# A decoder kernel: the values' first block product placed behind the gates' last one on TensorE

## The chip, the cores and the metric

One core of a Trainium2 chip runs the kernel. The core has five engines that run side by side, each with its own queue of instructions that it works through in order: TensorE (PE, matrix products; its weight loads are listed apart as PEld), VectorE (DVE), ScalarE (ACT), GpSimd (POOL) and SyncE (SP), which issues transfers. They meet through semaphores. The metric is the time of one execution on the device in microseconds.

## The reference

The kernel computes two layers of a decoder on 512 tokens of width 1024, in float32. The part that matters here is the retention branch of a layer, with its gates and values:

```
z = rmsnorm(x, g_mix) @ w_in                # split into ... rq, rk, rv, rg, ga, gb
r = chunkwise_retention(rotate(rq), rotate(rk) * 128 ** -0.5, rv)   # 4 heads, values 256 wide
r = r * rsqrt(mean(r * r, -1) + eps)
yb = (r.reshape(B, S, 1024) * silu(rg)) @ w_b
x = x + (sigmoid(ga) * (A @ w_a) + sigmoid(gb) * yb) @ w_out
```

rg are the retention's gates and rv its values; each is one block of 1024 columns of the combined projection. A is the attention's output.

## The kernel before, in words

Every float32 product is done as three matmuls on rounded parts: each operand is split into hi (a rounded copy, ScalarE, L342 for weights) and lo (the rest, VectorE, L343), and hi x hi, hi x lo and lo x hi are added up in PSUM. The function products (L394 to L396) issues such triples and keeps its last matmul in latest[0].

Weights come in units of 128 x 1024, in the fixed order of unit_order. A call of unit() hands out the next unit and, with it, traces the split of the unit three places ahead (SPLIT = 3) and the load of one four further on (AHEAD = 4). The split tiles hi and lo have four buffers each, so a new split waits until the products of an older unit are done.

Some large products are made from seven smaller block products in place of eight. For the gates' second half this is last_gates, for the values it is values. Both hold three accumulators: a, b and c (one PSUM bank each in last_gates, two each in values; the pool ps_mm has five banks, ps_aux three). Each has seven calls of multiply: a from the first quarter of the inputs; b begins as ScalarE's copy of a; c and b take products with combinations of the inputs that the class Turned has built before; keep copies a bank away with ScalarE; put reads a bank with VectorE and writes a result. Later multiplies go on adding into the same bank, so such a reader stands between two products. In last_gates a multiply is 24 matmuls of 128 x 256 (L1015) with one unit of weights; in values it is 24 matmuls of 128 x 512 with two units.

The order in last_gates is: a; copy to b; c; keep(c) (L1026); b; keep(b); a; put(0, 0) (L1036); c; put(0, 1) (L1033 and L1034); the silu of two gates (L1062, L1063); b; put(1, 1) (L1033, L1034); b; put(1, 0). In values the first call is multiply(a, quarter(0, 0)), which needs only the scaled inputs xh and xl and the first two units of values' weights; then come the copies of a into b (L969) and the second call, on c. A dummy matmul (L929) opens one of the banks of b.

A layer calls last_gates and then values directly after it; before them is the product with w_a (group w_a, 128 x 512), after them the projections qk(2) and qk(3), with the retention of the first two heads drawn in beside them.

The order in the code is not the order in the queues. After tracing, a planner runs the program forward in a simulated time of its own: on each engine it takes, among the instructions whose operands and buffers are ready, the one that was traced first. The result is each engine's fixed queue. An instruction that waits in that queue holds up all behind it. The context issue_after(ins) adds an edge of order only: what is traced inside it, on the engine of ins, comes behind ins in that queue. Instructions for other engines that are traced inside are not bound.

Of the kernel before, what the change touches and what calls it, by code (L numbers as in the profile page):

```python
# [111 lines left out]
def view(slot):  # L112
    return slot[0][:, slot[1], :]
# [3 lines left out]
def decoder(ctx, tc, xT, x_first, w_in, w_rg, w_rv, w_a, w_b, w_wo, w_up, w_pair, w_down, w_end, tables, decay, band, g_last, out):  # L117
    nc = tc.nc
# [10 lines left out]
    def f32(ap):  # L129
        return ap.bitcast(F32)  # L130

    def temp(name="t"):
        return tmp.tile([P, T], F32, tag="t", name=name, bufs=7)
# [4 lines left out]
    def bank(pool, name):  # L138
        return pool.tile([P, T], F32, tag=pool.name, name=name)
# [112 lines left out]
    def pace(src):  # L252

        if quiet[0]:
            return
        pace_count[0] += 1
        if steps and pace_count[0] % 2 == 0:
            mark = small.tile([P, 1], F32, tag="mark", name="mark", bufs=2)
            ins = nc.gpsimd.tensor_copy(mark, src[:, 0:1])
            with tc.issue_after(ins.ins):  # L260
                if next(steps[0], DONE) is DONE:
                    steps.pop(0)
# [91 lines left out]
    def unit(name, layer):  # L354
        i = state["next"]
        assert order[i][:2] == (layer, name), (order[i], layer, name)
        state["next"] += 1
        hold = state["hold"]
        split_until(i + SPLIT + 1 if hold is None else max(i + 1, min(hold, i + SPLIT + 1)))
        return parts.pop(i)  # L360
# [27 lines left out]
    def products(ps, pairs, start, stop, resume=False):  # L388


        n = len(pairs)
        for i, ((ah, al), (bh, bl)) in enumerate(pairs):
            more = {"skip_group_check": True} if resume else {}
            nc.tensor.matmul(ps, ah, bh, start=start and i == 0, stop=False, **more)  # L394
            nc.tensor.matmul(ps, ah, bl, start=False, stop=False, **more)  # L395
            latest[0] = nc.tensor.matmul(ps, al, bh, start=False, stop=stop and i == n - 1, **more).ins  # L396

    latest, behind, spread = [None], [], []
# [15 lines left out]
    def split(hi, lo, src, scale=None):  # L414

        if scale is None:
            up = nc.scalar.activation(hi, src, AF.Copy)  # L417
            down = nc.vector.tensor_tensor(lo, src, f32(hi), ALU.subtract)  # L418
        else:
            up = nc.scalar.activation(hi, src, AF.Copy, scale=scale)  # L420
            down = nc.vector.scalar_tensor_tensor(lo, src, scale, f32(hi), ALU.mult, ALU.subtract)
        return up.ins, down.ins
# [198 lines left out]
    def layer_body(layer):  # L621
# [299 lines left out]
        def quarter(half, tokens):  # L921
            at = slice(tokens * H, tokens * H + H)
            return [(xh[:, k, at], xl[:, k, at]) for k in range(4 * half, 4 * half + 4)]

        def values(turned):

            a, c = ([bank(ps_mm, "rv") for _ in range(2)] for _ in range(2))
            b = [bank(pool, "rv") for pool in (ps_mm, ps_aux)]
            nc.tensor.matmul(b[1], ones, xh[:, 0, :], start=True, stop=True)  # L929
            plus, minus = rms_mix.columns, small.tile([P, NB], F32, tag="ncol", name="ncol", bufs=1)  # L930
            nc.vector.tensor_scalar(minus, plus, -1.0, None, ALU.mult)

            def multiply(ps, moving, start=True):
                for u in range(2):
                    hi, lo = unit("rv", layer)
                    for m in range(2):
                        at = slice(m * P, (m + 1) * P)
                        pairs = []
                        for k in range(2):
                            xh_, xl_ = moving[2 * u + k]  # L940
                            cols = slice(k * T, (k + 1) * T)
                            pairs.append(((xh_[:, at], xl_[:, at]), (hi[:, cols], lo[:, cols])))
                        products(ps[m], pairs, start and u == 0, u == 1, not start)

            def scale(j, m, sign):
                return (plus if sign > 0 else minus)[:, 2 * j + m : 2 * j + m + 1]

            def keep(j, ps, sign):
                got = []
                for m in range(2):  # L950
                    t = temp("kept")
                    nc.scalar.activation(t, ps[m], AF.Copy, scale=scale(j, m, sign))
                    got.append(t)
                return got

            def put(i, j, ps, sign, kept=None):
                for m in range(2):
                    hi, lo = slots.one(), slots.one()
                    if kept:
                        nc.vector.scalar_tensor_tensor(kept[m], ps[m], scale(j, m, sign), kept[m], ALU.mult, ALU.add)  # L960
                        split(view(hi), view(lo), kept[m])
                    else:
                        split(view(hi), view(lo), ps[m], scale(j, m, sign))
                    rv[i, 2 * j + m] = (hi, lo)
                    pace(f32(view(hi)))

            multiply(a, quarter(0, 0))
            for m in range(2):
                nc.scalar.activation(b[m], a[m], AF.Copy)  # L969
            multiply(c, turned[1])  # L970
            five = keep(1, c, -1)
            multiply(b, turned[2], False)
            turned.free(0)
            two = keep(1, b, 1)
            multiply(a, quarter(1, 0), False)
            quiet[0] = False
            put(0, 0, a, 1)
            multiply(c, quarter(1, 1), False)
            put(0, 1, c, 1, two)
            multiply(b, turned[3], False)  # L980
            put(1, 1, b, -1, five)
            multiply(b, turned[4], False)
            turned.free(1)
            put(1, 0, b, -1)
# [19 lines left out]
        def last_gates(turned):  # L1004

            a, b, c = (bank(ps_mm, "rg") for _ in range(3))
            two = [big("z") for _ in range(2)]

            def multiply(ps, moving, start=True):
                hi, lo = unit("rg", layer)  # L1010
                for k, (vh, vl) in enumerate(moving):
                    for n in range(2):
                        o, cols = ps[:, n * H : (n + 1) * H], slice((2 * k + n) * P, (2 * k + n + 1) * P)
                        for w, v in ((hi, vh), (hi, vl), (lo, vh)):
                            nc.tensor.matmul(  # L1015
                                o,
                                w[:, cols],
                                v,
                                start=start and k == 0 and n == 0 and w is hi and v is vh,
                                stop=k == 3 and n == 1 and w is lo,  # L1020
                                skip_group_check=True,
                            )

            def keep(ps, sign):
                t = temp("kept")
                nc.scalar.activation(t, ps, AF.Copy, scale=float(sign))  # L1026
                return both(t)

            def put(i, j, ps, sign, kept=None):
                v = two[i][:, :, TOKENS[j]]  # L1030
                by = rstd()[:, TOKENS[j]].unsqueeze(1).broadcast_to([P, 2, H])
                if kept is not None:
                    nc.vector.scalar_tensor_tensor(kept, both(ps), float(sign), kept, ALU.mult, ALU.add)  # L1033
                    nc.vector.tensor_tensor(v, kept, by, ALU.mult)  # L1034
                else:
                    nc.vector.scalar_tensor_tensor(v, both(ps), float(sign), by, ALU.mult, ALU.mult)  # L1036

            def done(i):
                for m in range(2):
                    rg[4 + 2 * i + m] = two[i][:, m, :]  # L1040
                    silu(4 + 2 * i + m)

            multiply(a, quarter(0, 0))
            nc.scalar.activation(b, a, AF.Copy)
            multiply(c, turned[1])
            five = keep(c, -1)
            multiply(b, turned[2], False)
            sum_two = keep(b, 1)
            multiply(a, quarter(1, 0), False)
            put(0, 0, a, 1)  # L1050
            multiply(c, quarter(1, 1), False)
            put(0, 1, c, 1, sum_two)
            done(0)
            multiply(b, turned[3], False)
            put(1, 1, b, -1, five)
            multiply(b, turned[4], False)
            put(1, 0, b, -1)
            done(1)
# [954 lines left out]
```

## Time and profile before

| | |
|---|---|
| median of 3 runs | 1460.27 us (1459.97 to 1462.33) |
| the profiled execution, its own time | 1461.38 us |
| its span, first to last instruction | 1459.6 us |
| TensorE busy | 1447.5 us |
| VectorE busy | 1183.1 us |
| ScalarE busy | 976.5 us |
| GpSimd busy | 222.1 us |
| mean granted clock of TensorE | 0.999 |

Rows of a timeline give the start in us from the span's start, the duration, the engine, the line, the operation, what is written from what, the shape and a count; in brackets stands the idle time of the engine before the row and what ended it. Matmuls overlap in their pipeline: one of 128 x 256 shows 0.28 us but the next starts 0.12 us after it. In the groups by line, busy time and the mean in ns come first, then the idle time before. A granted clock of 1.00, or a digit 9, is full speed. The two blocks lie at 172.9 to about 227 us in layer 0 and at 895.3 to about 950 us in layer 1.

### The profile page before, as it was taken

What the parts mean: (1) busy time and instruction counts of PE and PEld (TensorE: products, weight loads), DVE (VectorE), ACT (ScalarE), POOL (GpSimd) and SP (SyncE); (2) the same over time, 40 slices, a digit from 0 to 9 for tenths busy, and PEclk for the clock granted to TensorE, in tenths of its full rate; (3) what the DMA queues carried; (4) which work ended last, traced back from release to release, by engine and by line L of the source; (5) the groups of instructions that cost most, each with busy time, mean ns of one, the idle gap of its engine ahead of it and who ended that gap; (6) DMA issues with size and microseconds to landing.
All of it is one profiled execution on the core that took longest, in us unless ns stands there. A gap on an engine that the chain in (4) does not pass through costs nothing.

```text
span 1459.6 us, 22457 instructions
## 1 busy us (share of the span) xinstructions
PE 1447.5 (99%) x8185; PEld 1269.5 (87%) x8185; DVE 1183.1 (81%) x1776; ACT 976.5 (67%) x1593; POOL 222.1 (15%) x335
## 2 busy tenths in 40 slices
PE   9999999999999999999999999999999999999998
PEld 7888888888989999999888888888889899999997
DVE  6977987877898888888778789878688888888885
ACT  6656665543688777777756576655447887777775
POOL 0021002221101111112201110021210011111120
PEclk9999999999999999999999999999999999999999
DMA  7598349999735777666955974499965477777764
GB/s 259 178 292 221 118 134 302 286 275 283 212 115 200 196 190 194 174 178 182 305 174 185 287 201 155 147 314 283 274 185 170 144 196 201 196 189 200 177 188 143
DMA packets 97294, 302.83 MB, mean 207 GB/s; under 512 B 11424, under 2 KB 11552, under 8 KB 90784
## 3 DMA queue, kind: packets, MB, share of 16 engines
q0 software_dynamic: 36512, 129.78, 38.0%
q1 hardware_dynamic: 59952, 170.32, 33.9%
q8 instruction: 64, 1.05, 0.3%
q10 hardware_dynamic: 720, 1.31, 0.2%
q14 instruction: 46, 0.38, 0.1%
HBM read 261.78 MB, written 120.06 MB: 262 GB/s over the span
## 4 chain that ended last, share of the span: by engine, by line
PE 95%; DVE 2%; ACT 1%; issue 0%; DMA 0%; DVEq 0%
PE mm L394 22%; PE mm L396 22%; PE mm L395 22%; PE wo L1354 5%; PE b L394 3%; PE b L395 3%; PE b L396 3%; PE rg L1015 2%; PE rv L394 2%; PE rv L395 2%; PE rv L396 2%; PE mm L410 2%; PE score L780 1%; PE pT L745 1%; PE r L395 1%; PE r L396 1%
## 5 line engine op out<-in xcount | busy, mean ns | idle before, releaser
L342 ACT ACTIVATE hi<-raw 128x1024 fp32r<-128x1024 f32 (+1 forms) x393 | 400.1, 1022 | 264.6 <-PE mm L395 118.4
L343 DVE TENSOR_TENSOR lo<-raw,hi 128x1024 fp32r<-128x1024 f32 (+1 forms) x394 | 459.3, 1175 | 103.1 <-ACT hi L342 101.5
L395 PE MATMUL mm<-xl,hi 128*128 128x512 f32 (+1 forms) x912 | 319.4, 353 | 0.0
L394 PE MATMUL mm<-xh,hi 128*128 128x512 f32 (+1 forms) x912 | 318.5, 353 | 0.7 <-ACT xh L420 0.7
L396 PE MATMUL mm<-xh,lo 128*128 128x512 f32 (+1 forms) x912 | 315.6, 352 | 0.0
L394 PEld LDWEIGHTS mm<-xh,hi 128*128 128x128 f32 x912 | 173.1, 190 | 23.3 <-ACT xh L420 1.4
L395 PEld LDWEIGHTS mm<-xl,hi 128*128 128x128 f32 x912 | 173.3, 190 | 21.9
L396 PEld LDWEIGHTS mm<-xh,lo 128*128 128x128 f32 x912 | 171.9, 190 | 21.4
L395 PE MATMUL mm<-r,hi 128*128 128x256 f32 (+1 forms) x608 | 189.2, 311 | 0.0
L396 PE MATMUL mm<-r,lo 128*128 128x256 f32 (+1 forms) x608 | 189.0, 311 | 0.0
L394 PE MATMUL mm<-r,hi 128*128 128x256 f32 (+1 forms) x608 | 186.9, 311 | 0.5 <-ACT mm L1529 0.5
L394 PEld LDWEIGHTS mm<-r,hi 128*128 128x128 f32 x608 | 115.7, 190 | 9.1 <-ACT mm L1529 0.7
L395 PEld LDWEIGHTS mm<-r,hi 128*128 128x128 f32 x608 | 115.7, 190 | 8.5 <-DVE r L418 0.4
L396 PEld LDWEIGHTS mm<-r,lo 128*128 128x128 f32 x608 | 115.8, 190 | 6.3
L1679 POOL DMA_DIRECT2D y<-eu x56 | 63.2, 1407 | 368.0 <-DVE eu L1662 367.6
L395 PE MATMUL mm<-lo,r 128*128 128x512 f32 (+1 forms) x276 | 104.4, 388 | 0.0
L396 PE MATMUL mm<-hi,r 128*128 128x512 f32 (+1 forms) x276 | 101.2, 387 | 0.2 <-DVE r L418 0.2
L394 PE MATMUL mm<-hi,r 128*128 128x512 f32 (+1 forms) x276 | 98.2, 389 | 0.3 <-ACT r L417 0.2
L394 PE MATMUL b<-hi,r 128*128 128x512 f32 x180 | 70.5, 391 | 0.0
L395 PE MATMUL b<-lo,r 128*128 128x512 f32 x180 | 70.2, 390 | 0.0
L1354 PE MATMUL wo<-r,hi 128*128 128x256 f32 x384 | 69.3, 283 | 0.0
L283 DVE TENSOR_TENSOR raw<-raw 128x512 f32<-128x512 f32 x56 | 38.5, 688 | 36.0 <-DMA raw<-w_pair_in 31.1
(337 smaller groups left out, 2865.5 us busy)
## 6 DMA issues: line engine op xcount, KB each, us to landing
raw<-w_in_in SPq DMA_DIRECT2D x65, 512.0 KB, 5.6
sums_down<-w_down_in POOLq DMA_DIRECT2D x30, 1024.0 KB, 12.2
sums_up<-w_pair_in POOLq DMA_DIRECT2D x56, 512.0 KB, 11.1
raw<-w_down_in SPq DMA_DIRECT2D x45, 512.0 KB, 7.2
raw<-w_pair_in SPq DMA_DIRECT2D x84, 256.0 KB, 3.6
y<-y POOLq DMA_DIRECT2D x62, 256.0 KB, 9.7
y<-eu POOLq DMA_DIRECT2D x61, 256.0 KB, 8.6
raw<-sums_down SPq DMA_DIRECT2D x30, 512.0 KB, 7.6
```

Of the source, the lines that this page charges most:

```text
L283: nc.vector.tensor_tensor(raws[i][:, at], last[:, LEFT], last[:, RIGHT], ALU.add)
L342: state["high"] = nc.scalar.activation(hi[:, at], raw[:, at], AF.Copy).ins
L343: nc.vector.tensor_tensor(lo[:, at], raw[:, at], f32(hi[:, at]), ALU.subtract)
L394: nc.tensor.matmul(ps, ah, bh, start=start and i == 0, stop=False, **more)
L395: nc.tensor.matmul(ps, ah, bl, start=False, stop=False, **more)
L396: latest[0] = nc.tensor.matmul(ps, al, bh, start=False, stop=stop and i == n - 1, **more).ins
L410: latest[0] = nc.tensor.matmul(ps, w[:, cols(j, c)], moving[k][low], start=first, stop=bool(final)).ins
L745: nc.tensor.transpose(pt[:, i * P : (i + 1) * P], sm[:, at : at + P], ident)
L780: nc.tensor.matmul(ps[:, g * w : (g + 1) * w], q_s[g][:, c, at], part[:, keys], start=i == 0, stop=i == 1)
L1015: nc.tensor.matmul(o, w[:, cols], v, start=start and k == 0 and n == 0 and w is hi and v is vh, stop=k == 3 and n == 1 and w is lo, skip_g ...
L1354: latest[0] = nc.tensor.matmul(o, w[:, cols], v, start=start and first and n % 2 == 0 and w is hi and v is vh, stop=final and w is lo, ski ...
L1679: nc.gpsimd.dma_start(y[:, 2 * j + m, i * T : (i + 1) * T], t, **how)
```

## The change

The last matmul of every gates' product is now kept in latest[0], and the values' first product is traced inside issue_after(latest[0]). So the 24 matmuls of that product, in each of the two layers, come behind the last matmul of the gates' seventh product in TensorE's queue. The other six products of the values and the splits, copies and loads of both blocks are traced as before.

```
@@ values @@
-            multiply(a, quarter(0, 0))
+            with tc.issue_after(latest[0]):
+                multiply(a, quarter(0, 0))
             for m in range(2):
                 nc.scalar.activation(b[m], a[m], AF.Copy)
             multiply(c, turned[1])
@@ last_gates, multiply @@
                         for w, v in ((hi, vh), (hi, vl), (lo, vh)):
-                            nc.tensor.matmul(
+                            latest[0] = nc.tensor.matmul(
                                 o,
                                 w[:, cols],
                                 v,
                                 start=start and k == 0 and n == 0 and w is hi and v is vh,
                                 stop=k == 3 and n == 1 and w is lo,
                                 skip_group_check=True,
-                            )
+                            ).ins
```

More of the change, by code (lines that the diff above doesn't have):

```diff
@@ L965, in put @@
                     pace(f32(view(hi)))
-            multiply(a, quarter(0, 0))
+            with tc.issue_after(latest[0]):
+                multiply(a, quarter(0, 0))
             for m in range(2):
@@ L1014, in multiply @@
                         for w, v in ((hi, vh), (hi, vl), (lo, vh)):
-                            nc.tensor.matmul(
+                            latest[0] = nc.tensor.matmul(
                                 o,
@@ L1021, in multiply @@
                                 skip_group_check=True,
-                            )
+                            ).ins
             def keep(ps, sign):
```

## The prediction

> **What bounds the kernel now.** I read the page first, then the list of waits of TensorE, then the timeline around the two blocks that the change touches, engine by engine. The page:
>
> ```profile
> span 1459.6 us, 22457 instructions
> ...
> PE 1447.5 (99%) x8185; PEld 1269.5 (87%) x8185; DVE 1183.1 (81%) x1776; ACT 976.5 (67%) x1593; POOL 222.1 (15%) x335
> ...
> PEclk9999999999999999999999999999999999999999
> ...
> PE 95%; DVE 2%; ACT 1%; issue 0%; DMA 0%; DVEq 0%
> ```
>
> TensorE is the bound: busy in 99% of the span, at full granted clock in every slice, and 95% of the chain that ended last. A change of order moves the time only if it makes or fills a gap on TensorE. The list of its waits, whole span first, then 200 to 720 us, then 925 us to the end (engine, line, what it waited for: us in total, times, longest):
>
> ```profile
> PE rv L394 <- ACT hi L342: 2.1, 2, 1.0
> ...
> PE mm L394 <- ACT mm L1529: 0.5, 1, 0.5
> PE mm L394 <- ACT r L417: 0.2, 1, 0.2
> PE wo L1354 <- ACT xh L420: 0.2, 1, 0.2
> ...
> PE mm L396 <- DVE r L418: 0.2, 1, 0.2
> ```
>
> The largest entry lies in this change's place, once in each layer. What follows the two blocks holds 0.9 us of waits in layer 0 and 0.2 us in layer 1, so a delay made here is hardly taken up later.
>
> TensorE in layer 0 (start, duration, line, operands, and in brackets the idle time before). The gates' seven products, 24 matmuls each, are rg L1015; I number them 1 to 7 in the order of the code.
>
> ```profile
> 184.28 0.28 PE L1015 MATMUL rg<-r,lo 128*128 128x256 f32 x1
> 185.59 0.73 PE L394 MATMUL rv<-hi,xh 128*128 128x512 f32 x2 [1.03 <-ACT hi L342]
> 186.16 0.30 PE L1015 MATMUL rg<-xh,hi 128*128 128x256 f32 x1
> ...
> 191.81 0.28 PE L1015 MATMUL rg<-r,lo 128*128 128x256 f32 x1
> 191.93 0.40 PE L395 MATMUL rv<-lo,xh 128*128 128x512 f32 x1
> ...
> 196.71 0.39 PE L396 MATMUL rv<-hi,xl 128*128 128x512 f32 x1
> 196.94 0.40 PE L1015 MATMUL rg<-r,hi 128*128 128x256 f32 x2
> ...
> 199.69 0.28 PE L1015 MATMUL rg<-r,lo 128*128 128x256 f32 x1
> 199.81 0.40 PE L394 MATMUL rv<-hi,r 128*128 128x512 f32 x1
> ```
>
> So the values' first product (24 matmuls) already runs inside the gates' block, in two pieces: 2 matmuls between the gates' third and fifth product (185.59), and 22 between the sixth and the seventh (191.93 to 196.94). The second piece costs TensorE no idle time. What it covers is seen on the other engines:
>
> ```profile
> 184.48 1.06 ACT L342 ACTIVATE hi<-raw 128x1024 fp32r<-128x1024 f32 x1 [0.26 <-PE rg L1015]
> 185.44 1.07 ACT L1026 ACTIVATE kept<-rg 128x512 f32<-128x512 f32 x2
> 186.07 0.19 PEld L1015 LDWEIGHTS rg<-xh,hi 128*128 128x128 f32 x1 [0.19 <-ACT kept L1026]
> ...
> 189.31 0.69 DVE L1033 SCALAR_TENSOR_TENSOR kept<-rg,kept 128x512 f32<-128x512 f32 x1 [2.05 <-PE rg L1015]
> ...
> 190.65 1.22 DVE L343 TENSOR_TENSOR lo<-raw,hi 128x1024 fp32r<-128x1024 f32 x1
> 191.79 0.68 DVE L1063 TENSOR_TENSOR z<-z,sig 128x512 f32<-128x512 f32 x1
> 192.39 0.68 DVE L1033 SCALAR_TENSOR_TENSOR kept<-rg,kept 128x512 f32<-128x512 f32 x1
> ```
>
> Products six and seven both accumulate into bank b, and put(1, 1) reads b in between: the second L1033, 192.39 to 193.07. The seventh product can't begin before that ends; 22 matmuls of the values stand there today.
>
> **The change part by part.** It adds no instruction and no semaphore, only an order on TensorE: the 24 matmuls of multiply(a) come behind the gates' last one. The block also traces splits and loads (ScalarE, VectorE, SyncE's queue), but the order binds TensorE's instructions alone, so these keep their queues. The assignment to latest[0] in the gates' block costs nothing; later readers of it come after other products have set it anew.
>
> *Gap one, at 184.56.* The gates' fifth product writes bank c, which keep(c) (L1026) must have read. ScalarE runs that copy behind the split of the values' first weights (184.48). The planner fills each queue forward in its own time, so up to the first matmul held back I take its queues as they are: split, then copy. The copy takes:
>
> ```profile
> L1026 ACT ACTIVATE kept<-rg x4: 580/586/592, 185.4 to 908.7; 128x512 f32<-128x512 f32 x4
> ```
>
> 185.44 + 0.58 = 186.02, and the weight load follows at 186.07, that is 0.05 us later. The fifth product thus starts at about 186.09 in place of 186.16: 0.07 us won. The two values' matmuls no longer stand in the gap; they are still to be done, at (196.94 - 191.93) / 22 = 0.228 each: 0.46 us lost.
>
> *Gap two, ahead of the seventh product.* Products five and six took 191.93 - 186.16 = 5.77, so they now issue until 186.09 + 5.77 = 191.86. L1033 stays at 192.39, since L1063 stands ahead of it on VectorE from 191.79, and ends at 193.07; with the same 0.05 the seventh product starts at 193.12. TensorE stands still for 193.12 - 191.86 = 1.26 us. Behind the waiting product are queued the whole values' block and everything after it. Two candidates could fill the gap. The values' second product needs weights whose split starts only after the sixth product frees its buffer, and the scores of the retention were already drawn forward as far as banks allow:
>
> ```profile
> 192.05 1.06 ACT L342 ACTIVATE hi<-raw 128x1024 fp32r<-128x1024 f32 x1
> ...
> 149.67 0.39 PE L929 MATMUL rv<-xh,ones 128*128 128x512 f32 x1
> 149.90 0.39 PE L394 MATMUL ret<-late 128*128 128x512 f32 x1
> ...
> 212.60 1.15 DVE L1092 TENSOR_TENSOR s<-ret,dm 128x512 f32<-128x512 f32 x2
> ```
>
> The split ends at 193.11, no earlier than the seventh product itself. Two score banks filled at 149.90 are read only at 212.60 and L929 took the third bank of that pool. Nothing fills the gap.
>
> *Check by the clock.* Seventh product 199.81 - 196.94 = 2.87, then 24 x 0.228 = 5.46: 193.12 + 2.87 + 5.46 = 201.45 for the start of the values' second product, against 199.81 today: +1.64 us, which is 0.46 - 0.07 + 1.26 within rounding. Layer 1:
>
> ```profile
> 908.35 0.73 PE L394 MATMUL rv<-hi,xh 128*128 128x512 f32 x2 [1.03 <-ACT hi L342]
> ...
> 914.68 0.40 PE L395 MATMUL rv<-lo,xh 128*128 128x512 f32 x1
> ...
> 922.57 0.40 PE L394 MATMUL rv<-hi,r 128*128 128x512 f32 x1
> ...
> 915.15 0.69 DVE L1033 SCALAR_TENSOR_TENSOR kept<-rg,kept 128x512 f32<-128x512 f32 x1
> ```
>
> 915.15 + 0.69 + 0.05 + 2.87 + 5.46 = 924.22 against 922.57: +1.65. Both layers show the same order and the same gap to a hundredth, so the plan goes by TensorE's pace here and not by chance. Sum: +3.29 us.
>
> *What moves behind it.* The copies of a into b (L969) come after a; the values' second product, 5.46 us, stands between them and their reader, and two such copies take under 1.2:
>
> ```profile
> 196.00 0.58 ACT L969 ACTIVATE rv<-rv 128x512 f32<-128x512 f32 x1 [0.47 <-PE rv L396]
> ```
>
> That row starts while the first product runs, since a[0] is complete before a[1]; I cost this at nothing, and 1.2 us a layer if the cover is gone. The splits of later units wait for buffers that free later, by up to 1.6 us, as does their reader. The loads behind them go through SyncE's queue; they have room:
>
> ```profile
> 172.90:199.80 26.90, 25.87 (x193) 24.60 (x192) 24.49 (x28) 16.89 (x22) 0.00 (x0) 1.00 0.42 136
> ```
>
> The DMA share in this stretch is 0.42, and GpSimd's column (the fifth, 0.00) shows no busy time, so its queue has no work here to be moved past. Bounds of gap two: from below, L1033 right after the sixth product. How fast VectorE answers TensorE is seen at the first L1033 and the last matmul of the fifth product:
>
> ```profile
> 188.93 0.28 PE L1015 MATMUL rg<-xh,lo 128*128 128x256 f32 x1
> ```
>
> It ends at 189.21, L1033 starts at 189.31: 0.10. So the second could start at 191.74 + 0.28 + 0.10 = 192.12, 0.27 earlier than in the sum (191.74 is the last matmul of today, 191.81, moved by 0.07). From above, one more split (1.14 apart on VectorE: 190.65 to 191.79) goes ahead of it. I take the row's own place, 192.39, and keep 0.99 to 2.40 for the range.
>
> [...] The window around gap one reads, in the view of TensorE alone:
>
> ```profile
> 184.30:186.20 1.90, 0.87 (x6) 1.00 0.35 108
> ```
>
> TensorE stood still for 1.03 us there and the granted clock stayed at 1.00; the new gap of 1.26 is little longer. If the clock were halved behind it, the seventh product would take 2.87 more in each layer, 5.74 in all, for 1469.3.
> [...]
>
> **The rivals.** *Gap two is cheaper*: the planner puts L1033 ahead of L1063. For it: L1033 is what the bound engine waits for. Against: the planner goes by what is ready, and L1063 was ready first in both layers. 3.29 - 2 x 0.27 = +2.75: 1463.0.
>
> *Not slower: the copy of c goes ahead of the split.* Its product, the second, starts at
>
> ```profile
> 175.76 0.40 PE L1015 MATMUL rg<-r,hi 128*128 128x256 f32 x2
> ```
>
> and is done 2.87 later, at about 178.7, long before the copy ran at 185.44. If the changed plan places it where the previous split ends (184.48 minus 0.26 idle: 184.22), product five starts at 184.22 + 0.58 + 0.05 = 184.85, which is 1.24 sooner, and all that follows moves with it: 1.64 - 1.24 = 0.40 a layer, 1461.1. It decides from 0.2 us a layer on, because the forecast stands only that far above the bound. Against it: the split and the copy both precede the first matmul held back. Were gap two filled as well, it would be 0.40 - 1.26 = -0.86 a layer, 1458.5; the gap there is to win, 2.06 us in all, is below what counts as faster.
>
> *A further wait in the values' block*, such as the copies of a into b behind a split whose buffer frees late: about one split (1.06) a layer, +5.4 in all, 1465.7. For it, ScalarE's waits from 172 to 200 us:
>
> ```profile
> ACT hi L342 <- PE rg L1015: 5.2, 5, 2.6
> ```
>
> Five splits stood at the head of ScalarE's queue until the gates' products freed a buffer, and what is behind such a split waits with it. Against it: the cover of 5.46 us.
>
> **How the numbers follow.** A change of 0.2% (2.92 us) is about what a measurement of this kernel can tell from none. The profiled execution took 1461.38 us, 1.78 around its span; with the sum it would be 1464.67. It stands 1.11 above the median of the runs, 1460.27, so the prediction is 1460.27 + 3.29 = 1463.6. Chances: the forecast (+2.9 to +3.7) 0.50, gap two cheaper 0.20, copy first 0.14, a further wait 0.11, half clock 0.02, faster for a reason not seen here 0.03. Slower by over 0.2%: 0.50 + 0.11 + 0.02, less 0.02 for the forecast's lower edge: 0.61. Within: 0.20 + 0.14 + 0.02 = 0.36. Faster: 0.03. The range from 1460.6 to 1466.2 takes in half of the copy-first case and the further wait. The likeliest alone: 1463.1 to 1464.0.
>
> **What would show it.** Right: 24 rv matmuls in a row behind the last L1015; L1015 waiting about 1.5 us for ACT L1026 and about 1.2 us for DVE L1033 in each layer, no rv wait for hi; the values' second product 1.6 us later relative to the gates' first. Wrong: L1026 ahead of the split at L342, other matmuls in gap two, or a new entry in the waits behind the blocks.

## The result, and the profile after

The changed kernel took 1464.98 us (median of 7 runs, 1463.73 to 1466.23), the kernel before 1460.27 (7 runs, 1459.34 to 1462.73): a ratio of 1.0028 with the 95% interval 1.0017 to 1.0039, so slower by 2.5 to 5.7 us. Run once more (e12 below) it was 1.0022, 1.0013 to 1.0031. The profiled execution took 1464.98 us with a span of 1463.2, 3.6 us above the span of before.

The page of the kernel after:

```profile
span 1463.2 us, 22461 instructions
...
PE 1448.0 (99%) x8185; PEld 1270.0 (87%) x8185; DVE 1183.0 (81%) x1776; ACT 976.1 (67%) x1593; POOL 229.1 (16%) x335
...
PEclk9999999999999999999999999999999999999999
```

TensorE's work is the same (1448.0 us against 1447.5), the clock is full; what was added is standing still. The page counts 22461 instructions, four more than before, with the same number of busy ones on every engine. The list of TensorE's waits (line, what it waited for: us in total, times, longest; line numbers behind the edit are one higher):

```profile
PE rg L1016 <- ACT kept L1027: 3.0, 2, 1.5
PE rg L1016 <- DVE kept L1034: 2.1, 2, 1.0
PE warm L374 <- DVE ones L369: 1.1, 1, 1.1
PE mm L394 <- ACT xh L420: 0.8, 1, 0.8
```

The wait of rv for hi is gone. In its place the gates' fifth product waits for the copy of bank c, 1.5 us in each layer, and the seventh for the read of bank b, 1.0 in each. Everything further down the list is as it was, to 0.1 us. TensorE's timeline in layer 0, and the rows of layer 1 that answer to it:

```profile
173.13 0.28 PE L1016 MATMUL rg<-xh,hi 128*128 128x256 f32 x1
...
184.52 0.28 PE L1016 MATMUL rg<-r,lo 128*128 128x256 f32 x1
186.31 0.39 PE L1016 MATMUL rg<-xh,hi 128*128 128x256 f32 x1 [1.52 <-ACT kept L1027]
...
192.05 0.28 PE L1016 MATMUL rg<-r,lo 128*128 128x256 f32 x1
193.38 0.51 PE L1016 MATMUL rg<-r,hi 128*128 128x256 f32 x2 [1.04 <-DVE kept L1034]
193.72 0.29 PE L1016 MATMUL rg<-r,lo 128*128 128x256 f32 x1
...
196.35 0.40 PE L394 MATMUL rv<-hi,xh 128*128 128x512 f32 x1
...
201.82 0.39 PE L394 MATMUL rv<-hi,r 128*128 128x512 f32 x1
...
897.24 0.28 PE L1016 MATMUL rg<-xh,hi 128*128 128x256 f32 x1
...
910.78 0.39 PE L1016 MATMUL rg<-xh,hi 128*128 128x256 f32 x1 [1.52 <-ACT kept L1027]
...
917.84 0.51 PE L1016 MATMUL rg<-r,hi 128*128 128x256 f32 x2 [1.04 <-DVE kept L1034]
...
926.29 0.39 PE L394 MATMUL rv<-hi,r 128*128 128x512 f32 x1
```

And the two rows of the other engines that end the waits, with the weight load that follows the second:

```profile
185.68 1.07 ACT L1027 ACTIVATE kept<-rg 128x512 f32<-128x512 f32 x2
...
192.64 0.68 DVE L1034 SCALAR_TENSOR_TENSOR kept<-rg,kept 128x512 f32<-128x512 f32 x1
...
193.37 0.30 PEld L1016 LDWEIGHTS rg<-r,hi 128*128 128x128 f32 x2 [1.25 <-DVE kept L1034]
```

The stretch from the gates' first matmul to the first matmul of the values' second product, called the block from here on, lasted 201.82 - 173.13 = 28.69 us. In the kernel before it ran from

```profile
172.89 0.28 PE L1015 MATMUL rg<-xh,hi 128*128 128x256 f32 x1
...
895.28 0.28 PE L1015 MATMUL rg<-xh,hi 128*128 128x256 f32 x1
```

to 199.81 (shown in the prediction), 26.92 us. Layer 1 has 926.29 - 897.24 = 29.05 against 922.57 - 895.28 = 27.29. So 1.77 and 1.76 us were lost here, 3.53 of the 3.6 us by which the spans differ.

### The profile page after: what moved, and what is told of

Same layout as the page of the kernel before. It is cut to its first block, busy times and chain, and to the rows that moved or that the text cites. A ratio compares the mean times of both kernels' runs of the same rounds, so it can differ in the third digit from the quotient of the medians.

```text
span 1463.2 us, 22461 instructions
## 1 busy us (share of the span) xinstructions
PE 1448.0 (99%) x8185; PEld 1270.0 (87%) x8185; DVE 1183.0 (81%) x1776; ACT 976.1 (67%) x1593; POOL 229.1 (16%) x335
## 4 chain that ended last, share of the span: by engine, by line
PE 95%; DVE 3%; ACT 1%; issue 1%; DMA 0%; DVEq 0%
PE mm L394 22%; PE mm L396 22%; PE mm L395 22%; PE wo L1355 5%; PE b L394 3%; PE b L395 3%; PE b L396 3%; PE rg L1016 2%; PE rv L394 2%; PE rv L396 2%; PE rv L395 2%; PE mm L410 2%; PE score L780 1%; PE pT L745 1%; DVE lo L343 1%; PE r L396 1%
```

## The experiments

The block repeats to a few hundredths between executions where nothing in it was changed, while whole runs scatter by 2 to 4 us. So each run was judged first by its block and its waits, and then by its time. All in one table (us; the difference is that of the block to the kernel before; the ratio is to the kernel before on the same chip, with its 95% interval):

| | block, layer 0 | layer 1 | difference, both layers | median | ratio |
|---|---|---|---|---|---|
| before | 26.92 | 27.29 | | 1460.27 | |
| changed | 28.69 | 29.05 | +3.53 | 1464.98 | 1.0028 (1.0017 to 1.0039) |
| e1 behind the sixth product | 27.38 | 27.71 | +0.88 | 1461.83 | 1.0004 (0.9996 to 1.0013) |
| e2 changed, copy of c ahead of a split | 27.78 | 28.16 | +1.73 | 1462.90 | 1.0012 (1.0003 to 1.0021) |
| e3 before, copy of c ahead of that split | 26.54 | 26.90 | -0.77 | 1459.88 | 0.9995 (0.9986 to 1.0004) |
| e4 before, copy ahead of two more splits | 26.54 | 26.92 | -0.75 | 1461.19 | 0.9997 (0.9988 to 1.0006) |
| e5 changed, second read of b | 33.42 | 32.78 | +11.99 | 1472.72 | 1.0073 (1.0061 to 1.0086) |
| e6 before, second read of b | 26.93 | 27.30 | +0.02 | 1460.22 | 0.9998 (0.9989 to 1.0006) |
| e7 changed, own bank for the seventh | 27.15 | 27.51 | +0.45 | 1460.52 | 0.9996 (0.9988 to 1.0005) |
| e8 changed, read ahead of the silu | 28.42 | 28.79 | +3.00 | 1464.52 | 1.0017 (1.0008 to 1.0026) |
| e9 before, c's late half first | 26.56 | 27.02 | -0.63 | 1460.06 | 0.9997 (0.9988 to 1.0005) |
| e10 the same, its inputs split first | 26.44 | 26.43 | -1.34 | 1459.06 | 0.9988 (0.9979 to 0.9997) |
| e11 the same, copy ahead of a split | 25.63 | 25.99 | -2.59 | 1457.92 | 0.9983 (0.9974 to 0.9991) |
| e12 changed, again | 28.68 | 29.04 | +3.51 | 1463.91 | 1.0022 (1.0013 to 1.0031) |

**e1: which gap costs what.** The order is taken from the sixth product:

```
             multiply(b, turned[3], False)
+            sixth[:] = latest
             put(1, 1, b, -1, five)
...
-            with tc.issue_after(latest[0]):
+            with tc.issue_after(sixth[0]):
                 multiply(a, quarter(0, 0))
```

> The changed kernel, but the values' first product is ordered behind the gates' sixth product in place of the seventh. Theory of the two gaps: the gap ahead of the seventh product is covered by all 24 matmuls again and only the gap ahead of the fifth stays, with the two matmuls out of it: about +0.4 us a layer on the kernel before, 1461.1 us; TensorE waits about 1.5 us a layer for L1026's copy (a shifted line number) and not at all for the read by VectorE. Rival, that holding the product back costs by what it does to the queues of the values' block further on: the product is still held back past the fifth and sixth, so a good part of the +3.3 to +4.7 us stays, 1463 or more.

On TensorE all 24 matmuls of the values' first product now stood between the sixth and the seventh. The list of waits has one entry of the block left:

```profile
PE rg L1018 <- ACT kept L1029: 3.0, 2, 1.5
```

The block is 0.46 and 0.42 us longer than before, the two matmuls of 0.228 that left the first gap. So of the 1.77 us a layer 1.3 belong to the gap ahead of the seventh product. The rival, a price for holding the product back as such, falls: past the fifth and sixth product it costs nothing beyond those two matmuls.

**e7: the second gap taken away with the order kept.** The seventh product gets a bank of its own:

```
+            four = keep(b, 1)
-            multiply(b, turned[4], False)
-            put(1, 0, b, -1)
+            multiply(d, turned[4])
+            nc.vector.tensor_tensor(four, both(d), four, ALU.add)
+            ...                     # v = -four * by, as put(1, 0) did
```

> The changed kernel, but the gates' seventh product goes into a bank of its own, and its sum with bank b is made on VectorE after a copy of b by ScalarE (one copy and one addition more in each layer). The order on TensorE is that of the changed kernel. Two gaps: the seventh product no longer waits for the read of b, so the gap of 1.26 us a layer is gone and only the one ahead of the fifth stays: 2.5 below the changed kernel, about 1462.4 by its median, 1461.1 by the sum on the kernel before. Rival, that the order itself costs (the values' first product late, the copies of a late): near 1465.

TensorE's rows of layer 0 around the wait that is left, and the first one of the values. The sixth and the seventh product now follow one another without a step:

```profile
182.51 0.40 PE L1016 MATMUL rg<-r,hi 128*128 128x256 f32 x2
184.19 0.39 PE L1016 MATMUL rg<-xh,hi 128*128 128x256 f32 x1 [1.28 <-ACT kept L1027]
...
192.68 0.40 PE L394 MATMUL rv<-hi,xh 128*128 128x512 f32 x1
```

The row at 182.51 holds the first two matmuls of the seventh product. Its bank is free, so the planner drew them into the gap ahead of the fifth product; in TensorE's queue they write into d. From 184.19 to 192.68 there are 8.49 us, for the 70 matmuls that are left of three products (0.12 each) and 0.1 at the first one. The fifth product itself starts no sooner than in the changed kernel: 184.19 - 171.00 = 13.19 us behind the gates' first matmul, against 186.31 - 173.13 = 13.18. Its listed wait is 1.28 in place of 1.52 only because the two matmuls, 0.24 us, stand in the gap; this was not foreseen. The block fell by 1.54 us a layer: 0.24 by these two, and 1.3 by the second gap. With the values' product where the change puts it, the loss is nearly gone: it was a wait for a bank, not the order.

**e5 and e6: the read made longer, without and with the cover.** One more read of b by VectorE, ahead of the one that counts:

```
             multiply(b, turned[3], False)
+            again = temp("again")
+            nc.vector.scalar_tensor_tensor(both(again), both(b), -1.0, five, ALU.mult, ALU.add)
             put(1, 1, b, -1, five)
```

> The changed kernel with one more read of bank b by VectorE between the sixth and the seventh product (its result is not used). By the order that the planner gives, the extra read, a product with the sigmoid and a split stand ahead of the read that counts, so this ends about 2.3 us later in each layer. Two gaps: the seventh product waits for it, TensorE's wait for VectorE grows from 1.0 to about 3.4 us a layer and the time by about 4.7, to 1469.7. Rival, that this wait is no part of the loss: the time stays near 1465.

> The kernel before with the same extra read. Two gaps: 22 matmuls of the values stand between the sixth and the seventh product for 5.0 us, and the later end of the read (about 3.5 us behind the sixth) lies within them: no wait on TensorE there, 1460.3 as before. Rival, that the extra work itself slows VectorE's queue and with it TensorE: +1 us or more here too.

In the kernel before the same work changed nothing: the block is 26.93 and 27.30, and the only wait in it is the old one:

```profile
183.80 0.73 PE L394 MATMUL rv<-hi,xh 128*128 128x512 f32 x2 [1.03 <-ACT hi L342]
```

In the changed kernel the wait grew to what was expected, 3.38 us, but the two blocks grew by 8.46 us in all, not by 4.7. TensorE in e5, layer 0: the first matmuls behind the gap, and the first of the values' product; then the view of time windows (stretch, its length, TensorE's busy time and matmuls, granted clock, share of the DMA engines, GB/s):

```profile
196.29 0.79 PE L1016 MATMUL rg<-r,hi 128*128 128x256 f32 x2 [3.38 <-DVE kept L1034]
196.89 0.41 PE L1016 MATMUL rg<-r,lo 128*128 128x256 f32 x1
...
201.58 0.46 PE L394 MATMUL rv<-hi,xh 128*128 128x512 f32 x1
```

```profile
193.90:194.90 1.00, 0.00 (x0) 0.99 0.00 0
194.90:195.90 1.00, 0.00 (x0) 0.50 0.00 0
...
200.90:201.90 1.00, 1.00 (x7) 0.59 0.00 0
201.90:202.90 1.00, 1.00 (x6) 1.00 0.00 0
...
924.20:925.20 1.00, 0.00 (x0) 1.00 0.00 0
925.20:926.20 1.00, 0.62 (x3) 0.57 0.00 0
...
928.20:929.20 1.00, 1.00 (x8) 0.72 0.83 287
```

The granted clock fell to 0.50 inside the gap, and the seventh product took 201.58 - 196.29 = 5.29 us in place of 196.35 - 193.38 = 2.97. So the 4.73 us by which the block of layer 0 grew are 2.34 of waiting and 2.32 of slow matmuls, to 0.07. In layer 1 the clock came back sooner, and the block grew by 3.73. What was expected of this run counted the wait alone; the clock was in the prediction as a rival with a chance of 0.02, at a gap of 1.26.

**e8: how much of the second gap is VectorE's queue.**

```
-            done(0)
             multiply(b, turned[3], False)
             put(1, 1, b, -1, five)
+            with tc.issue_after(reads[1]):     # the read in put(1, 1)
+                done(0)
```

> The changed kernel, with the products of the silu put behind the read of bank b on VectorE. Two gaps, lower bound of the second: the read starts 0.2 us sooner in each layer, 0.4 below the changed kernel, near 1464.6, with TensorE's wait for VectorE at about 0.8 in place of 1.04. Rival, that the read is held by VectorE's queue and not by the product: 0.6 us a layer, 1463.8.

```profile
193.31 0.50 PE L1016 MATMUL rg<-r,hi 128*128 128x256 f32 x2 [0.78 <-DVE kept L1036]
```

0.78 in place of 1.04, and the block 0.27 and 0.26 us shorter: so much of the gap was VectorE's queue, as the prediction's lower bound had it (0.27). The remaining 0.78 is the read behind the end of its product: here VectorE stood idle for 0.25 us ahead of the read, until the product was done.

**e2, e3 and e4: the copy of c on ScalarE.** e2 is the changed kernel and e3 the kernel before, both with the split of the values' first weights behind the copy; copied[0] is the copy in keep(c). e4 is as e3, with the block put around multiply(b, turned[2], False), whose split is the one of the gates' sixth product, two units earlier (its expectation says one):

```
+            with tc.issue_after(copied[0]):
-            multiply(c, quarter(1, 1), False)
+                multiply(c, quarter(1, 1), False)
```

> The changed kernel, with the split of the values' first weights put behind the copy of bank c on ScalarE. Two gaps: the fifth product starts about 1.2 us sooner in each layer and all behind it too, so 2.4 below the changed kernel, near 1462.5; TensorE's wait for the copy falls from 1.5 to about 0.3 us a layer, the wait for VectorE stays at 1.0. Rival, that the copy is late for another reason than its place behind the split (its bank or buffer): the wait stays at 1.5 us and the time at the changed kernel's.

> The kernel before, with nothing but the split of the values' first weights put behind the copy of bank c. Two gaps: no weights of the values are ready when the fifth product is, so their first product goes whole into the place ahead of the seventh, and the 1.03 us of idle time becomes about 0.3: 0.85 us a layer below the kernel before, 1458.6. Rival, that the 1.03 us only moves to the next wait: the time stays at 1460.3.

> The kernel before, with the split one unit earlier (that of the gates' sixth product) put behind the copy of bank c, so the copy is done while the fourth and third products still run. Two gaps: no idle time is left ahead of the fifth product and the place ahead of the seventh stays covered, 1.2 us a layer below the kernel before, 1457.8. Rival, that the second copy (of bank b) now stops ScalarE and makes the sixth or seventh product wait for its weights: a new wait of 0.5 us or more for a split, and a time at or above that of the run with the later split.

The direction came as expected, the size did not. e2 gained 0.91 and 0.89 us a layer, not 1.2; e3 gained 0.38 and 0.39, not 0.85, and e4 0.38 and 0.37, not 1.2. All three keep a wait of 0.69. e4 shows why. ScalarE and TensorE in its layer 0:

```profile
182.56 0.60 ACT L1028 ACTIVATE kept<-rg 128x512 f32<-128x512 f32 x1 [3.65 <-PE rg L1015]
```

```profile
182.25 0.28 PE L1015 MATMUL rg<-r,lo 128*128 128x256 f32 x1
183.22 0.38 PE L1015 MATMUL rg<-xh,hi 128*128 128x256 f32 x1 [0.69 <-ACT kept L1028]
```

The copy stood at the head of ScalarE's queue for 3.65 us and began only when the last matmul ahead of the gap had ended, at 182.53. So bank c isn't complete before that. TensorE's queue says the same: the products on c and on b run in halves, as the inputs of Turned are built in two steps, and c's second half comes last. Written with the banks by name, from that queue (one matmul of c's second half in truth stands among b's):

```
12 matmuls  c <- first half of turned[1]
12 matmuls  b <- first half of turned[2]
24 matmuls  a <- quarter(1, 0)
12 matmuls  b <- second half of turned[2]
12 matmuls  c <- second half of turned[1]
            (the gap)
24 matmuls  c <- quarter(1, 1)
```

A wait of 0.69 us is then the least for this order: the copy's 0.6 and the two handovers.

**e9, e10 and e11: c's late half ahead of b's.** e9 puts the second half on b behind the last matmul on c; e10 also splits c's inputs ahead of b's; e11 also puts the split of the gates' last weights behind the copy. All three on the kernel before:

```
-            multiply(b, turned[2], False)
+            multiply(b, turned[2], False, final[0])   # its k >= 2 behind c's last matmul
...
+                first = split(hi[:, 0:2, :], lo[:, 0:2, :], b11)
+                with tc.issue_after(first[0]), tc.issue_after(first[1]):
+                    split(hi[:, 2:4, :], lo[:, 2:4, :], two)
...
+            with tc.issue_after(copied[0]):
+                multiply(a, quarter(1, 0), False)
```

> The kernel before, with the second half of the gates' third product (on bank b, the half that needs the inputs built last) ordered behind the second product (on bank c). In all runs so far the two products interleave by halves and c's last 12 matmuls are the last ones ahead of the gap. Theory that the gap ahead of the fifth product is the time to copy c out after its late end: b's 12 matmuls (1.45 us) now cover the copy, the 1.03 us of idle time there goes, though c's late half may now wait up to 0.6 us for VectorE's split of its inputs: a block of 26.2 to 26.4 us from the gates' first matmul to the values' second product, against 26.92 before, so 1.0 to 1.5 us below in all. Rival, that the place of the copy in ScalarE's queue sets the gap: 26.92 as before.

> The same, and the inputs that c's late half needs are split ahead of those of b's. If VectorE's split is what holds c's half then, the wait in front of it goes as well: a block of 25.6 to 25.9 us, 2.0 to 2.6 us a run below the kernel before, 1458.3. Rival: the split is bound by the sums ahead of it and not by the order of the two, so the block stays at the 26.2 to 26.4 of the run without this order.

> The last kernel (c's late half first, its inputs split first), and the split of the gates' last weights put behind the copy of bank c as well, so that the copy runs while b's late 12 matmuls do. If the remaining wait ahead of the fifth product (0.55 and 0.18 us) was the copy standing behind that split on ScalarE, it goes, and the block is 25.7 to 26.1 us in both layers, 2 us or more a run below the kernel before, 1458.5. Rival: the split put off makes a later product wait for its weights, and the block stays at 26.4.

Each took away one wait and showed the next, so that e9 and e10 gained less than expected and e11 what was expected. In e9 c's half waited for VectorE's split, 0.37 us in layer 0 and 0.83 in layer 1; in e10 that wait was gone and the fifth product waited 0.55 and 0.18 for the copy, which now stood behind a split. Their rows, with ScalarE's of e10:

```profile
182.30 0.38 PE L1018 MATMUL rg<-r,hi 128*128 128x256 f32 x1 [0.37 <-DVE r L418]
```

```profile
183.76 0.39 PE L1019 MATMUL rg<-xh,hi 128*128 128x256 f32 x1 [0.55 <-ACT kept L1030]
...
182.18 1.04 ACT L342 ACTIVATE hi<-raw 128x1024 fp32r<-128x1024 f32 x1
183.13 0.58 ACT L1030 ACTIVATE kept<-rg 128x512 f32<-128x512 f32 x1
```

In e11 the copy ran ahead of it, beside b's late matmuls, and the fifth product followed without a step:

```profile
181.83 0.58 ACT L1032 ACTIVATE kept<-rg 128x512 f32<-128x512 f32 x1
```

```profile
182.58 0.28 PE L1019 MATMUL rg<-r,lo 128*128 128x256 f32 x1
182.70 0.28 PE L1019 MATMUL rg<-xh,hi 128*128 128x256 f32 x1
```

The list of waits has no entry in the block in either layer, and the block is 1.29 and 1.30 us shorter than before. At 1457.92 us, ratio 0.9983 (0.9974 to 0.9991), e11 is faster than both kernels of this case.

**e12: the size of the loss.**

> The changed kernel once more, on the same chip as the run above, for the size of the loss: by the blocks' lengths in the two profiles 1.77 and 1.76 us, 3.5 us in all, the ratio near 1.0024; by the medians on record 4.7 us, 1.0032.

The blocks repeat the first profile's to 0.01 us. The ratio is 1.0022, so the two measurements together stand around the blocks' 3.5 us; the first median, 4.7 us above, was on the high side of it.

## Why the prediction was right

*What bounds the kernel*: right. Nothing behind the block took up the delay, as the short list of waits behind it said: 3.53 us arose in the two blocks and the spans differ by 3.6. Outside the blocks the two executions differ by 0.24 ahead of the first, by -0.05 between them and by -0.1 behind the second.

*The change itself*: the prediction said that it adds no instruction and no semaphore. The page counts four instructions more. None is of a kind that counts as busy, and no time of theirs shows: the terms below account for the blocks to 0.03 us.

*Gap one*: the number was right; one reading beside it, on which a rival rested, was wrong. Moved by the 0.24 us by which this execution came later to the block, the fifth product starts at 186.07, against 186.09 forecast. But the prediction read the 24 matmuls after 175.76 as the whole second product, done at 178.7. They are the first halves of two products. The copy of c did wait for the split ahead of it (e2 and e3: without that, 0.69 in place of 1.52), and it could never have run "long before". The forecast was not touched by this, since it took the copy's time from its row and not from the end of its product.

*Gap two*: right. The read of b ended as forecast and the seventh product started at 193.38 - 0.24 = 193.14, against 193.12. Nothing filled the gap. e1 and e7 show that this wait is some 1.3 of the 1.77 us.

*The sum*: 1.64 and 1.65 forecast, 1.77 and 1.76 measured. The term that was too small is the seventh product, 2.97 us in place of 2.87: its first two steps, 193.38 to 193.72, took 0.34, where matmuls behind one another step 0.12 each. The prediction took its 2.87 from a product that followed another without a wait. What remains is 0.03 in layer 0 and nothing in layer 1. The fifth product lost the same tenth behind its wait, but this only made the second gap shorter, 1.21 from step to step in place of 1.26, because the read of b came no later for it.

*The time*: 1463.6 forecast, 1464.98 and 1463.91 measured, both in the range; only the second lies in the narrow interval called the likeliest (1463.1 to 1464.0).

*What moves behind it*: right; the copies of a into b and the later splits made no wait, and no rival of that kind came up.

*The rivals*: that the gap would be cheaper by an earlier read did not happen by itself; made so in e8 it gives the 0.27 a layer that was worked out. The rival with the copy ahead was priced at 1.24 us a layer for the copy at 184.22; e2 shows 0.9, because of the late half of c. The half clock did not come at gaps of 1.52 and 1.04: the windows 184.5 to 186.5 and 192.0 to 193.6 of the changed kernel show a granted clock of 1.00. No run shows what a gap of 2.40, the prediction's upper bound of the second, would have done. In e5, at a gap of 3.38, the clock fell when TensorE had been idle for about 2.0 us in layer 0 (from 196.29 - 3.38 = 192.91 to the 194.9 of the windows), and in layer 1 about 3.1 us after the idle time began (from 922.20 to 925.3). The price put on it, 2.87 us a layer, was an estimate from the product's length at full clock; in e5 the slow matmuls cost 2.32 in layer 0.

## What to carry to other kernels

When a block product is moved out of another block's way, look at what it covered: here a reader of a bank between two products that add into it left a hole of 1.2 us on TensorE, as long as the read (0.68), its handovers and its wait in its own queue, and independent matmuls had filled it. Identify products by their bank and inputs and not by counting matmuls, since a planner may run two of them in halves. And a block's own length, from a first to a last matmul, tells tenths of a microsecond apart where whole runs scatter by several.

## What the runs showed that was not expected

A gap of 3.38 us cost far more than its length: in e5 the clock stayed at 0.50 until some 201.7 in layer 0, 6.8 us, and until some 928.8 in layer 1, 3.4 us. Gaps up to 1.52 us (1.52 and 1.04 in the changed kernel) cost their length and some 0.1 us at the first matmuls behind.

The idle time was 3.38 us in both layers, but by the windows the fall came about 2.0 us after it began in layer 0 and about 3.1 in layer 1, and full clock came back about 5.4 us after the seventh product's start in layer 0 (196.29 to 201.7) and 3.2 in layer 1 (925.58 to 928.8). What sets these times was not shown. No run has a gap between 1.52 and 3.38 us in the block, so none tells from which length on the clock falls.

The profiled executions reach the block between 170.9 and 173.7 us, and much of this arises at the very start, in code that no run changed. TensorE's first four weight products in the kernel before and in e1:

```profile
5.55 2.05 PE L394 MATMUL mm<-xh,hi 128*128 128x512 f32 x4 [0.70 <-ACT xh L420]
```

```profile
5.60 1.17 PE L394 MATMUL mm<-xh,hi 128*128 128x512 f32 x4 [0.83 <-ACT xh L420]
```

Four matmuls took 2.05 us in the one and 1.17 in the other, the next four 1.91 and 1.08, and the four after them 1.28 and 1.07. The view of windows gives a granted clock of 1.00 for both, but here it is no measurement: in the kernel before the trace's list of clock periods begins only at 9.51 us, and the view counts a stretch without a record as full. There the first matmuls step (7.39 - 5.55) / 4 = 0.46 us, twice the 0.228 at full clock; in e1 they step (6.60 - 5.60) / 4 = 0.25. The thirteenth matmul starts at 10.22 in the one and at 8.43 in the other, 1.79 apart, and the block at 172.89 and 171.08, 1.81 apart. The fourteen profiles fall into two groups: the block is reached at 170.9 to 171.5 in six executions and at 172.9 to 173.7 in eight. Of the five whose first rows are on record, e1 and e11 have the short first four matmuls (1.17 and 1.19 us) and are of the early group; the kernel before, the changed kernel and e12 have the long ones (2.05, 2.07, 2.05) and are of the late one. So the pace of the first matmuls, and not what a run changed in the block, sets most of this difference between those five, and the spans of two single executions can't be compared to better than about 2 us. What makes it slow or fast stays open.
